# Splitting the last output piece by token stream and starting layer 1 with the latent tokens

## The chip, the cores and the metric

The kernel runs on one core of one Trainium2 chip. The metric is the device time of one execution in microseconds (us). The engines are named as the profile names them: PE (TensorE, matmuls), PEld (its weight loads), DVE (VectorE), ACT (ScalarE), POOL (GpSimd) and SP (SyncE, which issues nearly all the DMAs). Before the change three executions took 1798.65 to 1802.91 us, median 1800.26 us.

## What is computed

Two layers of a hybrid sequence model over 512 tokens of width 2048: 256 context tokens and 256 latent tokens. In each layer the tokens are normalised and modulated by vectors that come from a condition (`adaLN`, a large weight per layer), projected by one wide weight `w_in` into the inputs of four mixers (S5 state space, Hyena long convolution, retention, gated linear attention "GLA"), mixed, gated, projected back by `w_out` and added to the residual:

```python
for i in range(DEPTH):
    ctx_out = i < DEPTH - 1
    mod_l = silu(c) @ ada_w[i] + ada_b[i];  mod_c = silu(c_ctx) @ ada_w[i] + ada_b[i]
    h_l = rmsnorm(x_l, norm_w[i]) * (1 + sc_l) + sh_l      # 256 latent tokens
    h_c = rmsnorm(x_c, norm_w[i]) * (1 + sc_c) + sh_c      # 256 context tokens
    pl = project(h_l, w_in[i], all segments)
    pc = project(h_c, w_in[i], all segments if ctx_out else CTX_STATE_SEGMENTS)
    ... s5, hyena, retention, gla ...
    x_l = x_l + gt_l * (merged branches of the latents @ w_out[i])
    if ctx_out:
        x_c = x_c + gt_c * (merged branches of the context @ w_out[i])
return rmsnorm(x_l, final_norm_w)
```

In the last layer the context is needed only for the states that the latents start from, so its `gla_q` is not computed, while `s5_u` (512 columns) is computed for all 512 tokens and `gla_q` (256 columns) for the latents.

## The kernel before

**Matmuls in three products.** Each fp32 operand is kept as a high and a low part, and each product is hi·hi, hi·lo and lo·hi. The parts of the weights are made as they stream in: `wpart` (L944 on) loads 256 rows by 256 columns (256 KB) into a buffer `raw` (9 of them) by the DMA queue of SP, ACT casts it to `whi` (L935), and DVE subtracts to get `wlo` (L182); there are 6 buffers each of `whi` and `wlo`. The activations of a layer are 16 tiles of 128 features by 512 tokens, each as high and low part (`hs`).

**Buffers.** `tr` is a pool of 4 scratch tiles: modulated activations before they are split, products of the gate and the residual, and projections on the way to DRAM all take their turn in it. PSUM tiles are `pj` (3 buffers), `pA` and `pB` (2 each, asked for as `pm`), and `pa` (1).

**Last output piece.** `w_out` of layer 0 is done in 8 pieces of 256 columns (c = 0 to 7). A piece has 8 weight parts, and each part is used for 4 blocks of 128 tokens (0 and 1 context, 2 and 3 latent) by 6 matmuls of 256 columns, 192 matmuls in all. The four blocks end together at the last part. Each is multiplied by its gate and added to the residual (DVE, L182), its squares are summed (ACT, L1185), and after the last piece the features 14 and 15 are transposed on PE (L201), the four norm factors are spread over all partitions (`rrow`, L1195 on: DVE makes 4 diagonal tiles `junk`, PE multiplies them with ones), and `make_h` (L1211 on) makes the 16 modulated activation tiles of layer 1, all 512 tokens of a tile before the next.

**Start of layer 1.** `proj_wide` (L989 on) projects `s5_u`: 16 weight parts, each 12 matmuls of 512 columns, into two `pj` and two `pB` tiles. Behind each part, `step(2)` advances the background work `ada_gate(1, 't')` by two loads: 32 loads of 256 KB of `ada_w` in all, each with 4 small matmuls into `pa` (L197). Then come the S5 mixer (`s5_mix`), `gla_q` for the latents (`proj(1)`, 8 parts, 96 matmuls of 256 columns) and `gla_k` for all tokens (`proj(2)`, 512 columns a matmul), then the rest of the layer. While these run, a second background load of `ada_w` by DVE (`ada_el`, tile `acc`) goes on.

**Order.** The program text is not the order on the engines: a list scheduler (`schedule_with_timeline_sim=True`, L1610) builds the kernel with a model of its times and lays down one order for each engine, as the pools and the dependences permit. Each engine then runs its own row in order. A buffer of a pool is handed out in the order of the program text, whatever the scheduler does later.

The functions that the change touches are these.

Of the kernel before, what the change touches and what calls it, by code (L numbers as in the profile page):

```python
# [10 lines left out]
F32 = mybir.dt.float32  # L11
# [3 lines left out]
OP = mybir.AluOpType  # L15
# [101 lines left out]
class Net:  # L117
# [826 lines left out]
    def wpart(self, src, r0, c0, w, step=True, keep=False):  # L944

        raw = self.raw()[:, :, :w]
        self.nc.sync.dma_start(raw, src[r0:r0 + 256, c0:c0 + w].rearrange("(k p) c -> p k c", p=128))
        if keep:
            hi, lo = (self.tp.tile([128, 2, 256], F32R, name="m" + t, tag="m" + t, bufs=NM[t])[:, :, :w] for t in 'AB')
        else:  # L950
            hi, lo = self.whl('whi')[:, :, :w], self.whl('wlo')[:, :, :w]
        self.nw += 1
        self.split(hi, lo, raw, 'v')
        if step:
            self.due += self.rate
# [30 lines left out]
            for j in range(2):  # L986
                cb(a // 128 + j, ps[j])

    def proj_wide(self, W, c0, cb, steps):  # L989

        mark(f'pw@{c0}')
        self.cur, cur = 'B', self.cur
        ps = [self.pj(), self.pj(), self.pm(), self.pm()]
# [5 lines left out]
        for j in range(4):  # L999
            cb(j, ps[j])  # L1000

    def proj_n(self, W, c0, w, toks, cb, banks=None, order=range(8), step=True, keep=False):

        mark(f'pn{len(toks)}@{c0}')
        per = 1 if keep else 512 // w
        banks = [b() for b in banks or [self.pj] * (-(-len(toks) // per))]
        parts = {}

        def part(nq):
            if nq not in parts:  # L1010
                parts[nq] = self.wpart(W, order[nq] * 256, c0, w, step, keep)
# [24 lines left out]


    def silu_c(self):
# [157 lines left out]
    def rrow(self, rs):  # L1196
# [49 lines left out]
    def spill(self, dst, t0, scale=None):  # L1246
        def f(j, p):
            x = self.trt()
            if scale:
                self.nc.scalar.mul(x[:, t0:], p[:, t0:], scale)  # L1250
            else:
                self.cp(x[:, t0:], p[:, t0:], EV[j % 2])
            self.nc.sync.dma_start(dst[j * 128:(j + 1) * 128, t0:], x[:, t0:])
        return f

# [159 lines left out]

    WKQ = (0, 1, 6, 7, 4, 5, 2, 3)

    def w_out(self, i, c, toks, t0, x, gt, ss, step=True, done=None):

        cs = slice(c % 2 * 256, (c % 2 + 1) * 256)  # L1420
        mark(f'wout{i}')
# [1 line left out]
        def res(t, p):  # L1423
# [4 lines left out]
            self.sumsq(ss[:, t], c, xx)  # L1428
            if done:
                done(t)  # L1430
        self.proj_n(self.I['w_out'][i], c * 256, 256, toks, res, order=self.WKQ, step=step, keep=bool(done))

    def run(self, out):
        nc, I, tc = self.nc, self.I, self.tc
# [70 lines left out]
        for c in range(8):  # L1505
# [26 lines left out]
        rrow = self.rrow(self.rstd(ss))  # L1532
# [8 lines left out]
        self.layer(1, vec[1], Ps[1], kfd[1], lambda: nxt.update({0: self.gate_row(1, 0, 0)}))  # L1541
        x2 = {}

        def xl(t, c):
# [69 lines left out]
```

## Time and profile before

| | |
|---|---|
| three executions | 1798.65, 1800.26, 1802.91 us |
| the profiled execution | 1800.95 us |
| its span (first to last instruction) | 1799.1 us |
| mean granted clock of PE | 0.984 |
| busy: PE, DVE, ACT, POOL | 1728.2, 1234.9, 739.1, 127.0 us |
| DMA moved | 355.20 MB, mean 197 GB/s |

A row of the page or of an answer about the trace names an operation as line, engine, operation and `out<-in`, with sizes as partitions by elements. PE works for 96% of the span, so a stretch is read by where PE does not work, and by the clock that it is granted: 1.00 stands for 2.4 GHz, 0.50 for 1.2 GHz. Matmuls overlap in their records (a matmul of 256 columns has a duration of 0.28 us, and 252 in a row take 29.91 us), so costs are taken from stretches with a count and not from single durations. The profile is of one execution.

### The profile page before, as it was taken

What the parts mean: (1) busy time and instruction counts of PE and PEld (TensorE: products, weight loads), DVE (VectorE), ACT (ScalarE), POOL (GpSimd) and SP (SyncE); (2) the same over time, 40 slices, a digit from 0 to 9 for tenths busy, and PEclk for the clock granted to TensorE, in tenths of its full rate; (3) what the DMA queues carried; (4) which work ended last, traced back from release to release, by engine and by line L of the source; (5) the groups of instructions that cost most, each with busy time, mean ns of one, the idle gap of its engine ahead of it and who ended that gap; (6) DMA issues with size and microseconds to landing.
All of it is one profiled execution on the core that took longest, in us unless ns stands there. A gap on an engine that the chain in (4) does not pass through costs nothing.

```text
span 1799.1 us, 33742 instructions
## 1 busy us (share of the span) xinstructions
PE 1728.2 (96%) x12560; PEld 1416.5 (79%) x12560; DVE 1234.9 (69%) x2495; ACT 739.1 (41%) x1460; POOL 127.0 (7%) x200
## 2 busy tenths in 40 slices
PE   7997999999999999999899999899999999999997
PEld 4654668888776667876689899777897888999997
DVE  2462876568997784976697564368867688677764
ACT  5331235245336344231242433334355565554554
POOL 4001000000000000000022122000000000000133
PEclk9999999999999999999999999999999999999999
DMA  9766666557556476676885564449654345887963
GB/s 300 247 214 171 204 190 204 162 171 217 166 173 200 144 256 207 208 219 217 300 250 170 145 153 151 141 140 301 211 154 124 106 118 154 268 269 227 317 204 124
DMA packets 308029, 355.20 MB, mean 197 GB/s; under 512 B 42432, under 2 KB 227480, under 8 KB 307864
## 3 DMA queue, kind: packets, MB, share of 16 engines
q1 hardware_dynamic: 299936, 341.81, 62.3%
q10 hardware_dynamic: 5112, 8.79, 1.6%
q0 software_dynamic: 2816, 2.43, 0.7%
q8 instruction: 99, 1.62, 0.4%
q14 instruction: 66, 0.54, 0.1%
HBM read 316.11 MB, written 36.83 MB: 196 GB/s over the span
## 4 chain that ended last, share of the span: by engine, by line
PE 78%; DMA 11%; DVE 5%; ACT 2%; issue 1%; SPq 1%; POOL 0%; DVEq 0%; ACTq 0%; POOLq 0%
PE pj L197 32%; PE pj L1020 21%; PE pB L197 10%; PE pA L197 7%; DMA raw<-in_w_in_dram 4%; PE pa L197 4%; DMA raw<-in_ada_w_dram 2%; PE pB L201 2%; DVE mA L182 1%; PE pA L864 1%; DVE wlo L182 1%; PE pB L1020 1%; DMA kd<-mA 1%; DMA mA<-kd 1%; PE pA L201 1%
## 5 line engine op out<-in xcount | busy, mean ns | idle before, releaser
L197 PE MATMUL pj<-hs,whi 128*128 128x512 f32 (+1 forms) x2496 | 669.9, 355 | 4.4 <-ACT tr L175 3.7
L935 ACT CAST whi<-raw 128x512 fp32r<-128x512 f32 (+1 forms) x536 | 331.5, 621 | 699.2 <-DMA raw<-in_w_in_dram 329.9
L182 DVE TENSOR_TENSOR wlo<-raw,whi 128x512 fp32r<-128x512 f32 (+1 forms) x536 | 373.6, 703 | 302.6 <-ACT whi L935 286.7
L197 PEld LDWEIGHTS pj<-hs,whi 128*128 128x128 f32 x2496 | 432.3, 190 | 86.9 <-issue 21.5
L1020 PE MATMUL pj<-whi,hs 128*128 128x256 f32 (+1 forms) x2368 | 453.7, 289 | 1.2 <-DVE hs L182 1.2
L197 PE MATMUL pj<-hs,wlo 128*128 128x512 f32 (+1 forms) x1248 | 437.0, 353 | 0.2 <-DVE wlo L182 0.2
L1020 PEld LDWEIGHTS pj<-whi,hs 128*128 128x128 f32 x2368 | 372.1, 190 | 17.7 <-issue 15.6
L1020 PE MATMUL pj<-wlo,hs 128*128 128x256 f32 (+1 forms) x1184 | 338.5, 286 | 0.0
L197 PEld LDWEIGHTS pj<-hs,wlo 128*128 128x128 f32 x1248 | 236.4, 190 | 39.3 <-issue 10.0
L1020 PEld LDWEIGHTS pj<-wlo,hs 128*128 128x128 f32 x1184 | 224.5, 190 | 5.7 <-issue 5.2
L182 DVE TENSOR_TENSOR mA<-mA 128x512 f32<-128x512 f32 (+6 forms) x342 | 181.3, 558 | 29.2 <-DMA mA<-rq 12.6
L194 DVE SCALAR_TENSOR_TENSOR acc<-raw,sc,acc 128x512 f32<-128x512 f32 x210 | 153.6, 753 | 10.4 <-DMA raw<-in_ada_w_dram 9.8
L197 PE MATMUL pA<-mA 128*64 128x64 f32 (+4 forms) x892 | 123.2, 302 | 2.9 <-DMA mA<-in_s_glu_w_dram 1.7
L197 PE MATMUL pB<-hs,whi 128*128 128x512 f32 x320 | 104.4, 408 | 9.6 <-ACT whi L935 9.6
L197 PE MATMUL pa<-raw,sc 128*32 128x256 f32 (+1 forms) x1152 | 99.2, 369 | 9.8 <-DMA raw<-in_ada_w_dram 7.8
L197 PE MATMUL pB<-mB 64*64 64x128 f32 (+4 forms) x896 | 95.6, 297 | 10.0 <-DVE mB L182 7.7
L197 PEld LDWEIGHTS pA<-mA 128*64 128x64 f32 (+2 forms) x892 | 75.7, 161 | 26.7 <-issue 13.9
L197 PEld LDWEIGHTS pB<-mB 64*64 64x64 f32 (+2 forms) x896 | 61.5, 154 | 32.1 <-issue 12.3
L175 ACT COPY mA<-pA 128x512 f32<-128x512 f32 (+3 forms) x126 | 50.2, 420 | 88.7 <-PE pA L197 42.2
L197 PEld LDWEIGHTS pa<-raw,sc 128*32 128x32 f32 x1152 | 36.9, 110 | 59.3 <-issue 34.4
L197 PEld LDWEIGHTS pB<-hs,whi 128*128 128x128 f32 x320 | 60.3, 192 | 28.6 <-ACT whi L935 11.0
L182 DVE TENSOR_TENSOR mB<-mB 128x512 f32<-128x512 f32 (+2 forms) x140 | 65.6, 508 | 18.0 <-ACT mB L299 12.2
(230 smaller groups left out, 1587.6 us busy)
## 6 DMA issues: line engine op xcount, KB each, us to landing
raw<-in_ada_w_dram SPq DMA_DIRECT2D x384, 256.0 KB, 3.8
raw<-in_w_in_dram SPq DMA_DIRECT2D x384, 256.0 KB, 3.6
raw<-in_w_out_dram SPq DMA_DIRECT2D x128, 256.0 KB, 3.3
raw<-in_w_in_dram SPq DMA_DIRECT2D x32, 272.0 KB, 3.5
mB<-kfd SPq DMA_DIRECT2D x24, 256.0 KB, 4.8
mB<-in_ctx_dram SPq DMA_DIRECT2D x16, 256.0 KB, 5.5
mB<-in_x_dram SPq DMA_DIRECT2D x16, 256.0 KB, 6.0
kfd<-mA SPq DMA_DIRECT2D x16, 256.0 KB, 2.7
```

Source lines behind the costliest of these rows:

```text
L175: self.nc.scalar.copy(out, in_)
L182: (self.nc.vector if eng == 'v' else self.nc.gpsimd).tensor_tensor(out, a, b, op=op)
L194: self.nc.vector.scalar_tensor_tensor(out, in0, scalar, in1, op0=op0, op1=op1)
L197: self.nc.tensor.matmul(out, lhsT, rhs, start=start, stop=stop)
L201: self.nc.tensor.transpose(out, in_, self.K['ident'][:p, :p])
L864: nc.tensor.matmul(o, a_, b_, start=part == 0 and q < per, stop=part == 2, skip_group_check=True)
L935: self.nc.scalar.copy(hi, x)
L1020: mm = lambda a, b, start, stop: self.nc.tensor.matmul(o, a, b, start=start, stop=stop, skip_group_check=per > 1)
```

## The change

The piece c = 7 of `w_out` of layer 0 is done in two groups of token blocks, first 2 and 3 (latent), then 0 and 1 (context). Its 8 weight parts are kept for the second group: two of them in `mA` tiles of another pool, six in the `whi` and `wlo` buffers. After each group `half` does the transposes, the norm factors and `rrow` for these 256 tokens. The scale vectors of all 16 features are made in one instruction (`acols`), ahead of the piece.

Layer 1 begins with `proj_lat` on the latents: in each of 8 rounds two parts of `s5_u` and one of `gla_q`, 12 matmuls of 256 columns each (288 in all), with no background loads, and with the modulation of two features for the latents (`make_h_part`) at the round's start. Then `proj_lat` does `s5_u` for the context: 8 rounds of two parts (192 matmuls of 256 columns), the modulation for the context, and two background loads behind each part. So the 16 weight parts of `s5_u` are loaded and split twice. The results go to four tiles `ux` by ACT copies, and from there to DRAM; `proj(1)` is gone, its result is spilled at the end of the latent phase.

```diff
-    def proj_wide(self, W, c0, cb, steps):
...
+    def proj_lat(self, W, units, steps, before, ts):
...
+        ps = [self.pj() if ts.start else self.pm() for _ in units]
...
         for kq in range(8):
-            for a in range(2):
-                self.proj_part(W, kq, c0 + a * 256, ps[2 * a:2 * a + 2], 0, kq == 0, kq == 7, False)
+            before(kq)
+            for (c0, j0, cb), p in zip(units, ps):
+                hi, lo = self.wpart(W, kq * 256, c0, 256, False)
+                for j in range(2):
+                    cs = slice(j * 128, (j + 1) * 128)
+                    o = p[:, j * 256:(j + 1) * 256]
...
+                    for k in range(2):
+                        xh, xl = self.hh[kq * 2 + k][:, ts], self.hl[kq * 2 + k][:, ts]
+                        mm(hi[:, k, cs], xh, kq == 0 and k == 0 and j == 0, False)
+                        mm(hi[:, k, cs], xl, False, False)
+                        mm(lo[:, k, cs], xh, False, kq == 7 and k == 1)
                 self.step(steps)
...
-        for nq in range(8):
-            for n in range(len(toks)):
-                block(nq, n)
-        for n in range(len(toks)):
-            out(n)
+        groups = [range(len(toks))] if half is None else [range(0, 2), range(2, 4)]
+        for ns in groups:
+            for nq in range(8):
+                for n in ns:
+                    block(nq, n)
+            for n in ns:
+                out(n)
+            if half:
+                half(ns[0] // 2)
...
+    def make_h_part(self, k, x, m, acols, rrow, v, ts):
...
+        f = self.trt()
+        f = f[:, ts]
+        self.stt(f, x[:, ts], acols[:, k, v:v + 1], rrow[:, ts], op0=OP.mult, op1=OP.mult)
...
+        self.nc.scalar.activation(hi, f, AF.Identity, bias=b)
+        self.stt(lo, f, b, hi.bitcast(F32), op0=OP.add, op1=OP.subtract)
...
-            self.proj_wide(W, OFF[units[0][0]], units[0][3], 2)
+            ux = [self.t2() for _ in range(4)]
+            part = lambda ts: lambda j, p: self.cp(ux[j][:, ts], p)
+            two = lambda cb: [(OFF['s5_u'] + a, a // 128, cb) for a in (0, 256)]
+            self.proj_lat(W, two(part(slice(256, 512))) + [(OFF['gla_q'], 0, units[1][3])], 0, before_lat, slice(256, 512))
+            self.proj_lat(W, two(part(slice(0, 256))), 2, before_ctx, slice(0, 256))
+            for j in range(4):
+                units[0][3](j, ux[j])
         self.cur = 'A'
         self.s5_mix(i, P, vec, self.ud, lat, put)
         if lat:
-            proj(1)
             proj(2)
...
+        def half(h):
+            toks = (2, 3) if h == 0 else (0, 1)
...
+            for k in (14, 15):
+                p = self.pm()
+                for n, t in enumerate(toks):
+                    self.tr(p[:, n * 128:(n + 1) * 128], x1[t, 3][:, (k % 4) * 128:(k % 4 + 1) * 128])
...
+            self.rrow_part(rrow, sl[h], self.rstd(ss[:, toks[0]:toks[1] + 1]))
...
+        self.w_out(0, 7, (2, 3, 0, 1), 0, x0, gt, ss, False, half=half)
         self.hh, self.hl = [], []
-        for k in range(KT):
-            self.make_h(k, xT[k], m[1], vec[1], rrow)
+
+        def before(h):
+            def f(kq):
+                for k in (2 * kq, 2 * kq + 1):
+                    self.make_h_part(k, xT[k], m[1], ac, rrow, h, sl[h])
+            return f
```

Up to the piece c = 7 the two kernels lay the same instructions in the same order, but for the scale vectors. Behind it, all of layer 1 is scheduled anew. Three places follow, before first and then after; line numbers of the changed kernel are its own.

PE at the end of the piece, before: the last `w_out` matmuls, then background matmuls (`pa`), the transposes (L201), the norm factors (`junk`), and the first matmuls of `s5_u` on 512 tokens.

```order
L1020 MATMUL pj<-wlo,hs 128x256
L1020 MATMUL pj<-whi,hs 128x256
L197 MATMUL pa<-raw,sc 32x256 x16
L201 MATMUL pB<-c_kc,mB 128x128 x4
L197 MATMUL pa<-raw,sc 32x256 x2
L201 MATMUL pB<-c_kc,mB 128x128 x2
L197 MATMUL pa<-raw,sc 32x256 x2
L201 MATMUL pB<-c_kc,mB 128x128 x2
L197 MATMUL pa<-raw,sc 32x256 x4
L197 MATMUL pA<-junk,c_kc 128x128 x4
L197 MATMUL pa<-raw,sc 32x256 x6
L197 MATMUL pj<-hs,whi 128x512 x2
```

PE at the same place now: the last context matmuls of the piece, the context's transposes, and the first matmuls of `s5_u` on 256 latents; L1031 is in `w_out`, L1002 in `proj_lat`.

```order
L1031 MATMUL pj<-whi,hs 128x256 x2
L1031 MATMUL pj<-wlo,hs 128x256
L1031 MATMUL pj<-whi,hs 128x256
L201 MATMUL pB<-c_kc,mB 128x128 x4
L1002 MATMUL pj<-hs,whi 128x256 x4
L1002 MATMUL pj<-hs,wlo 128x256
L1002 MATMUL pj<-hs,whi 128x256 x2
L1002 MATMUL pj<-hs,wlo 128x256
```

The background matmuls and the latents' transposes and factors stand no longer between the piece and layer 1; the latter lie inside the context group of the piece.

DVE at the end of the piece, before: the products of gate and residual (`tr<-pj,mA`), the sums (`mB<-mB,tr`), the norm factors and the modulation (`tr<-mB,acol,mA`).

```order
L182 TENSOR_TENSOR mB<-mB,tr 128x256
L182 TENSOR_TENSOR tr<-pj,mA 128x256
L182 TENSOR_TENSOR mB<-mB,tr 128x256
L177 COPY mB<-pB 128x512
L182 TENSOR_TENSOR wlo<-raw,whi 128x2x256
L1191 TENSOR_REDUCE xs_12040<-xss 128x4
L239 RECIPROCAL xrs<-xrs 128x4
L1201 TENSOR_SCALAR junk<-c_kc,xrs 128x128 x4
L194 SCALAR_TENSOR_TENSOR tr<-mB,acol,mA 128x256 x8
L194 SCALAR_TENSOR_TENSOR acol<-mod_147,vec 128x2
L194 SCALAR_TENSOR_TENSOR hs<-tr,mod_147,hs 128x256 x2
```

DVE at the same place now.

```order
L177 COPY mA<-pB 128x256
L182 TENSOR_TENSOR wlo<-raw,whi 128x2x256 x5
L182 TENSOR_TENSOR tr<-pj,mA 128x256
L182 TENSOR_TENSOR mB<-mB,tr 128x256
L182 TENSOR_TENSOR wlo<-raw,whi 128x2x256
L182 TENSOR_TENSOR tr<-pj,mA 128x256
L182 TENSOR_TENSOR mB<-mB,tr 128x256
L194 SCALAR_TENSOR_TENSOR tr<-mB,acols,mA 128x256 x3
L177 COPY mA<-pB 128x256
L1206 TENSOR_REDUCE xs_12060<-xss 128x2
L194 SCALAR_TENSOR_TENSOR tr<-mB,acols,mA 128x256
L194 SCALAR_TENSOR_TENSOR hs<-tr,mod_147,hs 128x256 x2
```

The modulation of the latents still begins behind the products and sums of the last token block; it is no longer behind the context's norm factors.

SP's DMA queue around the boundary, before: residual loads, then two loads of `ada_w` (L1063) for each weight part (L947).

```order
L1502 DMA mB<-in_ctx_dram 128x512 x2
L1502 DMA mB<-in_x_dram 128x512 x2
L1063 DMA raw<-in_ada_w_dram 128x512 x2
L947 DMA raw<-in_w_in_dram 128x2x256
L1063 DMA raw<-in_ada_w_dram 128x512 x2
```

SP at the same place now (L1078 loads `ada_w`).

```order
L1553 DMA mB<-in_x_dram 128x512 x2
L947 DMA raw<-in_w_in_dram 128x2x256 x6
L1593 DMA x1d<-mB 128x512 x2
L947 DMA raw<-in_w_in_dram 128x2x256 x16
L1078 DMA raw<-in_ada_w_dram 128x512 x2
L947 DMA raw<-in_w_in_dram 128x2x256
L1078 DMA raw<-in_ada_w_dram 128x512 x2
```

The 24 parts of the latent phase and one of the context phase are asked for first (some of the 16 and 6 rows), and the 32 background loads all stand among the 16 parts of the context phase, two by two.

ACT near the end of the projection `ret_v` of layer 1, before: activations of S5 and GLA with their table loads, a weight cast (L935), then the copies of `ret_v` out of PSUM (`tr<-pj`).

```order
L810 ACT_TABLE_LOAD
L810 ACTIVATE mA<-mA,hpi 128x256
L316 ACT_TABLE_LOAD
L316 ACTIVATE mB<-mB 128x256
L317 ACTIVATE mB<-mB 128x256
L935 CAST whi<-raw 128x2x256
L312 ACTIVATE mB<-mB 128x512
L175 COPY tr<-pj 128x256 x4
```

ACT at the same place now.

```order
L316 ACT_TABLE_LOAD
L316 ACTIVATE mB<-mB 128x256
L317 ACTIVATE mB<-mB 128x256
L312 ACTIVATE mB<-mB 128x512
L935 CAST whi<-raw 128x2x256 x2
L175 COPY mB<-pB 128x512
L935 CAST whi<-raw 128x2x256
L175 COPY mA<-pA 128x128
L935 CAST whi<-raw 128x2x256
L175 COPY mA<-pA 128x128
L175 COPY tr<-pj 128x256 x4
```

Four weight casts and three copies now stand between the activations and the copies of `ret_v`.

## Rows read from the trace of the kernel before

**Rows 1.** Windows at the boundary; columns: busy us per engine, PEclk, DMA share, GB/s.

```profile
1132.30:1155.97 23.67, 23.67 (x204) 23.54 (x207) 6.56 (x11) 8.09 (x19) 2.07 (x3) 1.00 0.30 87
1155.97:1174.11 18.14, 12.54 (x93) 5.36 (x93) 12.80 (x37) 7.72 (x21) 0.00 (x0) 0.91 0.85 274
1174.11:1222.12 48.01, 48.01 (x247) 36.42 (x245) 27.72 (x70) 18.32 (x39) 0.00 (x0) 1.00 0.45 135
1222.12:1240.52 18.40, 15.63 (x141) 14.34 (x138) 17.22 (x30) 6.29 (x13) 0.00 (x0) 0.91 0.99 321
```

**Rows 2.** Timeline of PE there: start, us, work, [idle before it and what ended it].

```profile
1163.64 0.63 PE L197 MATMUL pa<-raw,sc 128*32 128x256 f32 x4 [1.72 <-DMA raw<-in_ada_w_dram]
...
1167.98 1.21 PE L197 MATMUL pa<-raw,sc 128*32 128x256 f32 x8 [1.37 <-DMA raw<-in_ada_w_dram]
...
1170.96 1.22 PE L197 MATMUL pj<-hs,whi 128*128 128x512 f32 x2
```

**Rows 3.** Windows of 2 us there, columns as before.

```profile
1170.00:1172.00 2.00, 2.00 (x7) 1.00 (x8) 2.00 (x8) 1.08 (x3) 0.00 (x0) 0.50 1.06 369
1172.00:1174.00 2.00, 2.00 (x15) 0.75 (x13) 2.00 (x8) 0.00 (x0) 0.00 (x0) 0.67 0.78 270
```

**Rows 4.** Timeline of PE in the attention q stretch.

```profile
1230.77 0.41 PE L197 MATMUL pA<-mA,cbr 64*32 64x128 f32 x4 [1.77 <-DVE mA L182]
...
1240.52 0.63 PE L197 MATMUL pj<-hs,whi 128*128 128x512 f32 x2
```

**Rows 5.** Windows of 2 us in that stretch.

```profile
1230.00:1232.00 2.00, 1.03 (x7) 0.76 (x8) 2.00 (x5) 0.00 (x0) 0.00 (x0) 0.84 0.97 311
1232.00:1234.00 2.00, 2.00 (x10) 1.87 (x10) 2.00 (x4) 0.62 (x1) 0.00 (x0) 0.50 1.05 343
```

**Rows 6.** Chain of waits, two stretches: start, us, work and count.

```profile
1184.58 2.79 PE pj L197 x12
...
1207.65 1.00 PE pa L197 x16
...
1667.95 29.91 PE pj L197 x252
```

**Rows 7.** Window of the 252 matmuls of the last row above.

```profile
1667.95:1697.86 29.91, 29.91 (x255) 29.91 (x254) 21.69 (x46) 15.90 (x32) 0.43 (x1) 1.00 1.00 320
```

**Rows 8.** Timeline of DVE after the last output matmuls.

```profile
1157.14 0.42 DVE L182 TENSOR_TENSOR mB<-mB,tr 128x256 f32<-128x256 f32 x1
1157.48 0.42 DVE L182 TENSOR_TENSOR tr<-pj,mA 128x256 f32<-128x256 f32 x1
```

**Rows 9.** Groups by line from 1155.97 to 1240.52: busy us, mean ns | idle before, releasers.

```profile
L182 DVE TENSOR_TENSOR wlo<-raw,whi 128x512 fp32r<-128x512 f32 x22 | 15.0, 686 | 23.1 <-ACT whi L935 15.9 <-PE pB L197 7.3
...
L194 DVE SCALAR_TENSOR_TENSOR hs<-tr,mod,hs 128x256 fp32r<-128x256 f32 x32 | 14.0, 476 | 0.0
L1225 ACT ACTIVATE hs<-tr,mod 128x256 fp32r<-128x256 f32 x32 | 13.6, 497 | 3.9 <-DVE tr L194 3.9
L935 ACT CAST whi<-raw 128x512 fp32r<-128x512 f32 x22 | 13.6, 620 | 47.7 <-DMA raw<-in_w_in_dram 32.8 <-PE pj L197 6.1 <-DVE acc L194 5.9
...
L197 PE MATMUL pa<-raw,sc 128*32 128x256 f32 x128 | 11.8, 398 | 5.2 <-DMA raw<-in_ada_w_dram 5.2
```

**Rows 10.** Timeline of PE at the end of retention v.

```profile
1481.61 0.80 PE L197 MATMUL pj<-hs,whi 128*128 128x256 f32 x2 [3.67 <-ACT tr L175]
```

**Rows 11.** Timeline of ACT there.

```profile
1466.46 0.69 ACT L296 ACTIVATE mB<-pB,vec 128x512 f32<-128x512 f32 x1 [2.30 <-PE pB L197]
...
1468.66 1.28 ACT L299 ACT_TABLE_LOAD   x1
1469.95 0.63 ACT L299 ACTIVATE mB<-mB 128x512 f32<-128x512 f32 x1
...
1480.93 1.17 ACT L175 COPY tr<-pj 128x256 f32<-128x256 f32 x4
```

**Rows 12.** Window behind that wait.

```profile
1480.00:1490.00 10.00, 8.39 (x49) 8.39 (x49) 8.70 (x15) 5.59 (x12) 0.00 (x0) 0.66 0.56 159
```

More of the change, by code (lines that the diff above doesn't have):

```diff
@@ L948, in wpart @@
         if keep:
-            hi, lo = (self.tp.tile([128, 2, 256], F32R, name="m" + t, tag="m" + t, bufs=NM[t])[:, :, :w] for t in 'AB')
+            hi, lo = (self.tp.tile([128, 2, 256], F32R, name="m" + t, tag="m" + t, bufs=NM[t])[:, :, :w] for t in keep)
         else:
@@ L987, in proj_t, with proj_n @@
                 cb(a // 128 + j, ps[j])
-    def proj_wide(self, W, c0, cb, steps):
-        mark(f'pw@{c0}')
+    def proj_lat(self, W, units, steps, before, ts):
+        mark('plat')
         self.cur, cur = 'B', self.cur
-        ps = [self.pj(), self.pj(), self.pm(), self.pm()]
+        ps = [self.pj() if ts.start else self.pm() for _ in units]
         self.cur = cur
         for kq in range(8):
-            for a in range(2):
-                self.proj_part(W, kq, c0 + a * 256, ps[2 * a:2 * a + 2], 0, kq == 0, kq == 7, False)
+            before(kq)
[4 more added lines that the diff above has]
+                    o = p[:, j * 256:(j + 1) * 256]
+                    mm = lambda a, b, start, stop: self.nc.tensor.matmul(o, a, b, start=start, stop=stop, skip_group_check=True)
+                    for k in range(2):
[3 more added lines that the diff above has]
+                        mm(lo[:, k, cs], xh, False, kq == 7 and k == 1)
                 self.step(steps)
-        for j in range(4):
-            cb(j, ps[j])
-    def proj_n(self, W, c0, w, toks, cb, banks=None, order=range(8), step=True, keep=False):
+        for (c0, j0, cb), p in zip(units, ps):
+            for j in range(2):
+                cb(j0 + j, p[:, j * 256:(j + 1) * 256])
+    def proj_n(self, W, c0, w, toks, cb, banks=None, order=range(8), step=True, keep=False, half=None):
         mark(f'pn{len(toks)}@{c0}')
@@ L1010, in part @@
             if nq not in parts:
-                parts[nq] = self.wpart(W, order[nq] * 256, c0, w, step, keep)
+                parts[nq] = self.wpart(W, order[nq] * 256, c0, w, step, 'AB' if keep else 'AA' if half and nq < 2 else '')
             return parts[nq]
@@ L1205, in rrow, with rrow_part, acols @@
         return x
+    def rrow_part(self, x, ts, rs):
+        n = ts.stop - ts.start
+        p = self.pm()
+        for t in range(n // 128):
+            d = self.sm.tile([128, 128], F32, name="junk")
+            self.nc.vector.tensor_scalar(d, self.K['ident'], rs[:, t:t + 1], None, op0=OP.mult)
+            self.mm(p[:, t * 128:(t + 1) * 128], self.K['ones'], d)
+        self.cp(x[:, ts], p[:, :n])
+    def acols(self, m, vec):
+        a = self.sm.tile([128, 16, 2], F32, name="acols", bufs=1)
+        self.stt(a, m[:, 1], 1.0, vec[:, 0:16, None].to_broadcast([128, 16, 2]), op0=OP.add, op1=OP.mult)
+        return a
+    def make_h_part(self, k, x, m, acols, rrow, v, ts):
+        mark('makeh')
+        f = self.trt()
+        f = f[:, ts]
+        self.stt(f, x[:, ts], acols[:, k, v:v + 1], rrow[:, ts], op0=OP.mult, op1=OP.mult)
+        if len(self.hh) <= k:
+            self.hh.append(self.hs())
+            self.hl.append(self.hs())
+        hi, lo = self.hh[k][:, ts], self.hl[k][:, ts]
+        b = m[:, 0, k, v:v + 1]
+        self.nc.scalar.activation(hi, f, AF.Identity, bias=b)
+        self.stt(lo, f, b, hi.bitcast(F32), op0=OP.add, op1=OP.subtract)
     def warm_sqrt(self, ss):
@@ L1416, with w_out @@
     WKQ = (0, 1, 6, 7, 4, 5, 2, 3)
-    def w_out(self, i, c, toks, t0, x, gt, ss, step=True, done=None):
+    def w_out(self, i, c, toks, t0, x, gt, ss, step=True, done=None, half=None):
         cs = slice(c % 2 * 256, (c % 2 + 1) * 256)
@@ L1430, in res @@
                 done(t)
-        self.proj_n(self.I['w_out'][i], c * 256, 256, toks, res, order=self.WKQ, step=step, keep=bool(done))
+        self.proj_n(self.I['w_out'][i], c * 256, 256, toks, res, order=self.WKQ, step=step, keep=bool(done), half=half)
     def run(self, out):
@@ L1510, in run @@
                 self.warm_sqrt(ss)
+                break
             self.w_out(0, c, range(4), 0, x0, gt, ss, c < CS)
@@ L1540, in run @@
         self.bg = self.ada_gate(1, HOW[6:8])
-        self.layer(1, vec[1], Ps[1], kfd[1], lambda: nxt.update({0: self.gate_row(1, 0, 0)}))
+        self.layer(1, vec[1], Ps[1], kfd[1], lambda: nxt.update({0: self.gate_row(1, 0, 0)}),
+                   before(0), before(1))
         x2 = {}
```

23 lines of the change are left out of this document (19 added, 4 removed).

## The prediction

> **What bounds the kernel now.** I read first the share of PE (96% of the span), then windows around the place that the change touches, then PE's timeline there, then the chain of waits. The windows [rows 1] show four stretches. Up to 1155.97 us, the end of the last `w_out` matmuls, PE is full. In the next 18.14 us, from the residual to the first matmuls of `s5_u`, PE has 12.54 us of busy records at a mean clock of 0.91. Then come 48.01 us full at clock 1.00, and 18.40 us with `gla_q` in which PE has 15.63 us, DVE 17.22 us and the DMAs a share of 0.99. Everything else of layer 1 keeps its amount of work.
>
> How much of these 84.55 us is lost? Matmuls are priced by counted rows [rows 6]: 252 of 256 columns in 29.91 us are 0.1187 us each, 12 of 512 columns in 2.79 us are 0.2325, 16 background ones in 1.00 us are about 0.065. The work is 192 × 0.2325 = 44.6 for `s5_u`, 96 × 0.1187 = 11.4 for `gla_q`, 128 × 0.065 = 8.3 for the background [rows 9], and my estimate of 3.1 for transposes, factors and pieces of S5: 67.4 us. So about 17 us are lost: some 11 in the first stretch, where PE waits for loads of `ada_w` (1.72 and 1.37 us [rows 2]) that stand ahead of weights in SP's queue and then runs two windows at 0.50 and 0.67 [rows 3]; some 5 in the `gla_q` stretch, where a wait of 1.77 us on DVE's S5 work [rows 4] is followed by windows at 0.84 and 0.50 [rows 5]; 1 elsewhere.
>
> **The change, part by part.** I count from the same point, the last `w_out` matmul, to the first matmul of `gla_k`, which was at 1240.52 [rows 4].
>
> *The piece by halves.* It has the same 192 matmuls, and the latents' transposes and factors go into the context half, where PE is full (0.7 us of PE). But the modulation of the latents does not start there: its scratch tile comes from the pool of 4 that the residual products also use, so in DVE's order the first one stands behind the last context sum. What the change seems made to hide stays open. From the last matmul: products and sums of two blocks at 0.79 a block (0.34 + 0.45, from one add to the next [rows 8]) and a weight split at about 0.6 make 2.2; one modulation on DVE 0.48 and the high part on ACT 0.50 [rows 9] make 3.2; the low part, behind two more DVE instructions, adds 0.8. That is a gap of 4.0 us. Bounds: 2.8 if the first block's residual is done while the second still multiplies, 6 if the low parts come one by one behind all scratch copies.
>
> *Clock behind the gap.* After the wait of 1.77 us the clock cost about 1.3 us (0.32 + 1.0 in two windows [rows 5]), after a wait of 3.67 us 3.4 us (10 us at 0.66 [rows 10, 12]). The gap is nearest to the second: 3.4.
>
> *Latent phase.* 288 × 0.1187 = 34.2 us. Beside it, per round of 36 matmuls (4.3 us): DVE three splits at 0.69 and four modulation steps at 0.48, 4.0 us; ACT three casts at 0.62 and two high parts at 0.50, 2.9 us [rows 9]. DVE is close, but the records overlap by about a tenth, and the first parts are prepared during the piece, so I cost the cover as holding. If it doesn't, the phase is 2 us longer. 24 loads of 262 kB in 34 us are 185 GB/s, and no load of `ada_w` stands among them.
>
> *Context phase.* PE has 192 × 0.1187 = 22.8 and 128 × 0.065 = 8.3, 31 us. But all 32 background loads now stand here, two behind each of 16 weight parts; before, they had the 64 us from 1157 to 1222. The 9 `raw` buffers bound what can be fetched ahead: by the order, some 13 of the 48 loads (eight of `ada_w`, and weights that were already cast) when the latent phase ends, since `pa` matmuls stand behind it on PE. The other 35 come at the rate of a saturated stretch, 320 GB/s [rows 7], 0.82 us each: 28.7 us. PE's own start costs about 2.8 us more, since ACT has four copies and the spill of `gla_q` ahead of the next cast and a scratch tile waits for the store; and the last load needs its landing, cast and split. I take 37 us. Bounds: 31 (PE alone decides) and 42 (the 274 GB/s of the second stretch [rows 1]: 35 × 0.96 = 33.5, and the same ends).
> The Trainium skill ("DMA: Bandwidth & Descriptors", Specifications) gives about 358 GB/s as a core's limit to its memory. By that the 35 loads would take an estimated 25.6 us and the phase end 3 us earlier. The saturated stretch shows 320 [rows 7], with 256 KB loads like these, and I keep to that.
>
> *Behind it.* The S5 input is complete some 12 us later than before. Its mixer is spread over the layer beside PE, and the long run of 252 matmuls at 1667.95 [rows 6] shows work that fills PE late, so I cost it at nothing; if that cover fails, it is part of the slower case. The S5 pieces that stood in the `gla_q` stretch (1.7 us) now come after `gla_k` begins and count in both. The doubled splits (16 casts, 16 subtractions) lie beside matmuls.
>
> The sum: 4.0 + 3.4 + 34.2 + 37 = 78.6, and 1.7 for the S5 pieces and 1.2 for transposes and factors that are done in both make 81.5, against 84.55: 3.1 us gained. In this the smaller matmuls cost 480 × 0.1187 − 44.6 − 11.4 = 1.0 us.
>
> *A stall far behind.* At the end of `ret_v` PE waits 3.67 us [rows 10] for copies by ACT that stand behind a block of S5 and GLA activations with five table loads, from 1466.46 to 1480.93 [rows 11], and the clock then costs 3.4 us [rows 12]. Now the copies stand farther behind that block, and PE has about 135 matmuls between the one that starts the block and the one that needs the copies, against 9.7 us before the wait: some 16 to 20 us, longer than the 14.5 us of the block. Then 7.1 us go. But all of the layer is laid anew, and another block may meet another wait: 0 to 7.1, and I take half, 3.5.
>
> Together 3.1 + 3.5 = 6.6 us. The profiled execution is 1800.95 us (span 1799.1), 0.7 above the median of 1800.26. 1800.95 − 6.6 = 1794.3 us.
>
> **Rivals.**
> *Faster than that* (1789 us): the context phase is bounded by PE alone (31 us, 6 less). For it: the DMAs idle at a share of 0.45 in the stretch of 48 us [rows 1] and may run further ahead. Against: nine buffers. Chance 0.13.
> *No change* (1800 us): the context phase takes 42 us and the stall of ACT only moves: 3.1 − 5 + 3.5 = 1.6 with half of it, −1.9 with none, about 0 between. For it: every stretch here that mixes `ada_w` with weights has PE waiting [rows 2, 5]. Against: the long stretch does not. Chance 0.26.
> *Slower* (1806 us): PE stops for loads of `ada_w` once in each round of the context phase, and the clock falls again and again. Rows 3 and 5 show 0.50 behind waits of 1.4 to 1.8 us. With half of the phase's 31 us of work at 1.2 GHz, that half takes 15 us more; about 3.5 of it covers waits that were there anyway, so 12 us are added. It decides as soon as most rounds have a wait of over 1.4 us, which 37 us against 31 does not yet give (6 us over 16 parts are 0.4 each). The Trainium skill ("TensorE: Matmul & The Clock Gate", HAM oscillation) tells of a loop in which short bursts of matmuls between waits for loads slow the clock in every turn; the windows here agree that the clock falls behind such waits, and no row shows it in turn after turn. Chance 0.17, with a new ACT collision or a late S5 counted in it.
> *Not what it says*: the overlap of modulation and context half does not happen, which is already in the sum.
>
> **How the numbers follow.** Forecast 0.44, faster rival 0.13, no change 0.26, slower 0.17. A measurement tells changes from about 0.2% (3.6 us). Faster by more: the faster rival, nearly all of the forecast (0.41 of 0.44) and a little of no change (0.02), 0.56. Within: 0.26 with 0.03 from the forecast, less 0.04 to the sides, 0.25. Slower: 0.19. The forecast's own range is 1790 to 1798 (terms 28.7 to 33.5, 0 to 7.1); reaching to the middle of the faster and the slower case it becomes 1787 to 1805.
>
> **What would show it.** Right: one gap of PE of about 4 us between the last `w_out` and the first latent matmul, then windows at 0.50; a full latent phase of 34 us; a context phase of about 37 us with the DMA share near 1.00, about 320 GB/s and PE's waits on loads of `ada_w` under 1 us; `gla_k` some 3 us earlier; no wait of 3 us on an ACT copy of `ret_v`. Wrong: a gap under 2 us (the overlap works after all) or a second wait between the phases; windows at 0.50 inside the context phase; PE full there; or a difference that grows behind `gla_k`, which would put the cause into the new order of the layer.

## The result and the profile after

The changed kernel is slower: 1813.2 us median of nine executions (1809.74 to 1819.31) against 1800.26 (nine, 1795.26 to 1810.3), ratio 1.0074 (95% interval 1.0055 to 1.0092), some 13 us. The forecast was 1794.3 us with a range of 1787 to 1805. The profiled execution has a span of 1807.9 us against 1799.1.

The last `w_out` matmul of layer 0 ends at a different point in each profile (here 1152.02, before 1155.97), so I count from its start, 1151.74 and 1155.69 us, and cut there and at the first matmul of `gla_k` (1234.04 and 1240.52): 82.3 us now against 84.8 before in the front, 573.9 against 558.6 behind it. The front gained 2.5 us, and 15.3 us were lost behind it, 12.8 us together. (The two spans differ by 8.8 us only, because up to that matmul the changed kernel's profile was already 4.0 us ahead.)

Windows of the changed kernel: the gap, the latent phase, the context phase, and the clock behind the gap (columns as in [rows 1]).

```profile
1152.02:1155.70 3.68, 0.85 (x4) 0.40 (x4) 3.57 (x9) 2.40 (x8) 0.00 (x0) 1.00 0.71 194
1155.70:1192.75 37.05, 36.59 (x292) 36.25 (x292) 27.39 (x58) 21.52 (x43) 0.00 (x0) 0.95 0.55 151
1192.75:1234.04 41.29, 40.16 (x322) 28.17 (x321) 21.54 (x45) 18.26 (x36) 0.00 (x0) 1.00 0.88 282
...
1156.00:1158.00 2.00, 1.54 (x11) 1.34 (x10) 2.00 (x7) 1.07 (x4) 0.00 (x0) 0.86 0.01 3
1158.00:1160.00 2.00, 2.00 (x11) 2.00 (x11) 2.00 (x7) 1.32 (x3) 0.00 (x0) 0.50 0.00 0
1160.00:1162.00 2.00, 2.00 (x16) 2.00 (x15) 2.00 (x6) 1.63 (x4) 0.00 (x0) 0.79 0.01 4
```

Behind the last output piece some 7 us were lost before: of 18.14 us PE was not busy for 5.6 [rows 1], and the clock cost 1.7 [rows 3]. Now there are a gap of 3.7 us and a slow clock that costs 1.7 us (0.28 + 1.00 + 0.42 over three windows). The latent phase is full. So is the context phase, nearly, at clock 1.00: not the DMAs bound it, but PE, which is busy for 40.2 of its 41.3 us. The background matmuls are the reason. Less 192 × 0.1187 = 22.8 us for `s5_u`, 17.4 us are left for 128 of them. Their own records (`pa` alone in that window) cover 14.63 us:

```profile
1192.75:1234.04 41.29, 14.63 (x128) 4.17 (x128) 0.00 (x0) 0.00 (x0) 1.00 0.88 282
```

The loss behind `gla_k` is one of waiting. Windows from `gla_k` to the first `w_out` of layer 1, before and after:

```profile
1240.52:1697.70 457.18, 449.71 (x3862) 404.88 (x3861) 346.82 (x670) 239.91 (x463) 4.17 (x20) 0.99 0.66 196
```

```profile
1234.04:1707.54 473.50, 452.76 (x3902) 407.21 (x3901) 361.89 (x696) 245.73 (x475) 5.26 (x20) 0.99 0.67 198
```

PE is not busy for 7.5 us of it before, of which 3.67 are the wait of [rows 10], and for 20.7 us in the changed kernel. Its waits there (us in total, times, longest):

```profile
PE pj L197 <- ACT tr L1454: 10.2, 1, 10.2
PE pA L864 <- DMA mA<-kd: 3.7, 3, 2.5
PE pB L201 <- DVE mB L182: 2.3, 1, 2.3
PE pA L201 <- DVE mA L182: 1.3, 1, 1.3
...
PE pj L197 <- ACT tr L175: 0.3, 1, 0.3
```

The stall at `ret_v` is gone, as forecast (0.3 us at most is left of the 3.67). But one wait of 10.2 us stands at the last gates (L1454). Its links, from the timelines of ACT, DVE, SP and PE of the changed kernel:

```profile
1666.10 0.32 SPq L1281 DMA_DIRECT2D ys<-mA  x1
...
1667.55 8.77 SPq L1433 DMA_DIRECT2D mA<-ys  x16
...
1672.59 2.37 DVE L182 TENSOR_TENSOR mA<-mA,mB 128x256 f32<-128x256 f32 x4 [7.48 <-DMA mA<-ys]
...
1675.39 0.78 ACT L1454 ACTIVATE tr<-pj 128x256 f32<-128x256 f32 x2 [8.01 <-DVE mA L194]
...
1675.83 0.79 PE L197 MATMUL pj<-hs,whi 128*128 128x256 f32 x2 [10.16 <-ACT tr L1454]
```

Read upwards: PE waits for a PSUM tile that ACT has to empty; ACT waits for one of the four `tr` tiles; DVE, which uses them up, waits for mixer outputs (`ys`) to come back from DRAM; and all 16 reloads stand in SP's queue behind the last store of retention, at 1666.10. Hyena's last store was already issued by then (`ys<-mB`):

```profile
1664.22 0.79 SPq L1281 DMA_DIRECT2D ys<-mB  x2
```

In the kernel before, on SP:

```profile
1653.46 0.41 SPq L1236 DMA_DIRECT2D ys<-mA  x1
...
1655.91 0.43 SPq L1382 DMA_DIRECT2D mA<-ys  x1
...
1660.38 4.59 SPq L1382 DMA_DIRECT2D mA<-ys  x9
...
1667.44 0.34 SPq L1236 DMA_DIRECT2D ys<-mB  x1
...
1676.03 0.42 SPq L1236 DMA_DIRECT2D ys<-mB  x1
```

There, too, all 16 reloads stand behind retention's last store. But that store, at 1653.46, comes 16.6 us earlier, counted from the last `w_out` matmul (497.8 against 514.4 us), and Hyena was not done: 12 reloads went out ahead of its last four stores (1667.44 to 1676.03), while it still gave PE work. Back along the chain, the first DRAM store of the S5 mixer (`kd<-mA`, L788), before and after:

```profile
1239.92 0.38 SPq L788 DMA_DIRECT2D kd<-mA  x1
```

```profile
1259.54 0.47 SPq L788 DMA_DIRECT2D kd<-mA  x1
```

From the last `w_out` matmul that is 84.2 us before and 107.8 us after. Before, S5 began while `gla_q` still ran, so that `gla_q` covered its first steps; now `gla_q` is done and S5's input is complete only with the context phase. On PE that input is complete 15.9 us later than before (82.3 against 66.4 us), and the first store comes 23.6 us later.

### The profile page after: what moved, and what is told of

Read it like the earlier page. It is cut to its first block, busy times and chain, and to the rows that moved or that the text cites. A ratio compares the mean times of both kernels' runs of the same rounds, so it can differ in the third digit from the quotient of the medians.

```text
span 1807.9 us, 34226 instructions
## 1 busy us (share of the span) xinstructions
PE 1730.2 (96%) x12752; PEld 1425.0 (79%) x12752; DVE 1247.0 (69%) x2499; ACT 754.3 (42%) x1488; POOL 126.7 (7%) x200
## 4 chain that ended last, share of the span: by engine, by line
PE 77%; DMA 10%; DVE 6%; ACT 3%; issue 2%; SPq 1%; POOL 0%; DVEq 0%; ACTq 0%; POOLq 0%
PE pj L197 30%; PE pj L1031 20%; PE pB L197 9%; PE pA L197 7%; PE pa L197 5%; DMA raw<-in_w_in_dram 4%; DVE mA L182 2%; PE pj L1002 2%; PE pB L1002 1%; DVE wlo L182 1%; DMA raw<-in_ada_w_dram 1%; PE pB L1031 1%; PE pA L864 1%; PE pB L201 1%; PE pA L201 1%
## 5 line engine op out<-in xcount | busy, mean ns | idle before, releaser
L197 PE MATMUL pj<-hs,whi 128*128 128x512 f32 (+1 forms) x2368 | 634.1, 355 | 12.0 <-ACT tr L1454 10.2
L935 ACT CAST whi<-raw 128x512 fp32r<-128x512 f32 (+1 forms) x550 | 339.8, 621 | 663.7 <-DMA raw<-in_w_in_dram 299.1
L182 DVE TENSOR_TENSOR wlo<-raw,whi 128x512 fp32r<-128x512 f32 (+1 forms) x550 | 385.8, 707 | 293.0 <-ACT whi L935 279.0
L197 PEld LDWEIGHTS pj<-hs,whi 128*128 128x128 f32 x2368 | 411.1, 191 | 91.0 <-issue 19.4
L1031 PE MATMUL pj<-whi,hs 128*128 128x256 f32 (+1 forms) x2336 | 445.4, 287 | 0.0
L197 PE MATMUL pj<-hs,wlo 128*128 128x512 f32 (+1 forms) x1184 | 416.0, 355 | 0.0
L1031 PEld LDWEIGHTS pj<-whi,hs 128*128 128x128 f32 x2336 | 365.2, 189 | 14.3 <-issue 13.1
L1031 PE MATMUL pj<-wlo,hs 128*128 128x256 f32 (+1 forms) x1168 | 332.2, 285 | 0.0
L197 PEld LDWEIGHTS pj<-hs,wlo 128*128 128x128 f32 x1184 | 224.7, 190 | 37.0 <-issue 9.0
L1031 PEld LDWEIGHTS pj<-wlo,hs 128*128 128x128 f32 x1168 | 219.9, 188 | 4.9 <-issue 4.7
L182 DVE TENSOR_TENSOR mA<-mA 128x512 f32<-128x512 f32 (+6 forms) x342 | 181.1, 559 | 27.9 <-DMA mA<-rq 10.2
L194 DVE SCALAR_TENSOR_TENSOR acc<-raw,sc,acc 128x512 f32<-128x512 f32 x210 | 154.2, 756 | 11.0 <-DMA raw<-in_ada_w_dram 10.3
L175 ACT COPY mA<-pA 128x512 f32<-128x512 f32 (+2 forms) x125 | 49.6, 420 | 101.7 <-PE pA L197 56.1
L197 PE MATMUL pB<-hs,whi 128*128 128x512 f32 x256 | 83.9, 412 | 6.8 <-ACT whi L935 6.8
L197 PEld LDWEIGHTS pB<-hs,whi 128*128 128x128 f32 x256 | 48.4, 194 | 23.3 <-ACT whi L935 8.2
```

What stands on the lines that cost most here:

```text
L175: self.nc.scalar.copy(out, in_)
L182: (self.nc.vector if eng == 'v' else self.nc.gpsimd).tensor_tensor(out, a, b, op=op)
L194: self.nc.vector.scalar_tensor_tensor(out, in0, scalar, in1, op0=op0, op1=op1)
L197: self.nc.tensor.matmul(out, lhsT, rhs, start=start, stop=stop)
L935: self.nc.scalar.copy(hi, x)
```

## The experiments

Theory A: S5 and retention follow one another (both take their scratch from `mA`, in program order), this chain is nearly critical in the kernel before, and the change starts it late. Theory B: only the new order of the reloads on SP is at fault. Theory C: the front itself costs the time. Theories D (a late S5 costs the same whatever the delay) and E (the background loads bind the context phase) came up on the way. For each kernel the time from the last `w_out` matmul (its start) to the end is split at S5's first store and at retention's last store, each from its own profile:

| kernel | to S5's first store | S5 and retention | from there to the end | sum | ratio to before (interval) |
|---|---|---|---|---|---|
| before | 84.2 | 413.5 | 145.6 | 643.4 | 1 |
| after | 107.8 | 406.6 | 141.8 | 656.2 | 1.0074 (1.0055 to 1.0092) |
| b_qfirst | 116.5 | 404.7 | 143.8 | 665.0 | 1.0112 (1.0083 to 1.0140) |
| b_qkfirst | 134.9 | 424.4 | 140.9 | 700.2 | 1.0328 (1.0292 to 1.0365) |
| a_qlast | 93.8 | 415.3 | 143.2 | 652.4 | 1.0050 (1.0029 to 1.0070) |
| a_ysq | 108.3 | 408.1 | 132.0 | 648.4 | 1.0020 (1.0001 to 1.0039) |
| a_steps | 107.9 | 416.7 | 140.3 | 664.9 | 1.0174 (1.0145 to 1.0204) |
| a_cut | 108.7 | 327.2 | 191.2 | 627.1 | 0.9922 (0.9895 to 0.9950) |
| b_cut | 83.6 | 342.0 | 206.8 | 632.4 | 0.9944 (0.9925 to 0.9964) |
| b_half | 78.8 | 414.4 | 147.7 | 640.9 | 0.9979 (0.9957 to 1.0000) |
| b_half_again | 80.2 | 415.6 | 147.0 | 642.8 | 0.9976 (0.9960 to 0.9993) |
| bh_ysq | 78.7 | 416.6 | 146.6 | 641.9 | 0.9977 (0.9959 to 0.9995) |
| bh_s1 | 69.8 | 425.7 | 148.8 | 644.3 | 1.0004 (0.9982 to 1.0025) |

b_half and b_half_again are one kernel, so a sum is good to some 2 us. What lies ahead of the last `w_out` matmul is in the ratios but not in the sums; it took 1149 to 1169 us in these profiles.

**b_qfirst**: S5 late without the split.

```diff
+            proj(1)
             self.proj_wide(W, OFF[units[0][0]], units[0][3], 2)
...
-            proj(1)
             proj(2)
```

> The kernel before, with gla_q projected ahead of s5_u instead of behind it: the same work, no split by streams, but the S5 mixer's input is complete some 18 us later against the start of gla_k. Theory A (the changed kernel lost its time because S5 starts late, the chain S5 then retention ends late, and PE runs out of other work before the last gates): S5's first store comes 15 to 20 us after the start of gla_k instead of at it, PE waits 5 to 12 us near the end of layer 1, and the time is 1805 to 1813 us, ratio 1.003 to 1.007. Theory B (only the order of the SP queue at the end is at fault, all 16 reloads of mixer outputs standing behind retention's last store; S5's lateness is innocent): in this kernel 12 of the reloads stand ahead of Hyena's last stores as before, so no long wait and 1797 to 1803 us, ratio 0.998 to 1.002.

Ratio 1.0112, more than A said. S5's first store comes 26 us behind the start of `gla_k`, and the part behind that start takes 574.7 us, as in the changed kernel (573.9). PE waits at the last gates though the reloads stand in nearly the old order (12 of them ahead of Hyena's last two stores):

```profile
1682.05 0.79 PE L197 MATMUL pj<-hs,whi 128*128 128x256 f32 x2 [6.67 <-ACT tr L1403]
```

B alone falls. The front costs 5.4 us besides (90.2 us), which I had not expected.

**a_qlast**: the split stays, `gla_q` back behind S5.

```diff
-            self.proj_lat(W, two(part(slice(256, 512))) + [(OFF['gla_q'], 0, units[1][3])], 0, before_lat, ...
+            self.proj_lat(W, two(part(slice(256, 512))), 0, before_lat, ...
...
+            proj(1)
             proj(2)
```

> The changed kernel, with gla_q taken out of the latent phase and projected behind the S5 mixer as before; the split by streams and the halved output piece stay. Theory A: S5's first store comes about at the start of gla_q, some 10 us earlier against the rest than in the changed kernel, retention's last store comes early enough, the wait of 10.2 us near the end shrinks to under 3 us, and the time is 1796 to 1803 us, ratio 0.998 to 1.002. Theory C (the front itself costs the time, by doubled splits and shorter matmuls): it stays at 1809 to 1814 us, ratio 1.005 to 1.008.

The time missed A's range, 1.0050. The part behind `gla_k`'s start (counted from where `gla_q` is done; two matmuls of `gla_k` stand ahead of that) is as A said, 557.3 us (558.6 before), and the wait at the gates is gone (4.1 us stand elsewhere). But the front takes 95.1 us, 10.3 more than before: a context phase of 42.2 us and a `gla_q` stretch of 22.6 us, of which PE is not busy for 4.8. So C holds for this kernel: without `gla_q` in the latent phase the split pays nothing and costs 10 us. In the table this loss, too, goes with S5's start: it is 9.6 us later than before, and the sum is 9.0 us larger.

Four kernels now differ only in whether they have the change's front and in where `gla_q` stands. With `gla_q` ahead of S5 the part behind `gla_k`'s start takes 574.7 us (old front) and 573.9 (new); with `gla_q` behind S5's input it takes 558.6 (old) and 557.3 (new). In the first two S5's first store comes some 26 us behind the start of `gla_k`, in the other two about 1 us ahead of it. So what is lost behind `gla_k` goes with S5's lateness and not with the split.

**a_ysq**: reloads off SP.

```diff
-            nc.sync.dma_start(o, self.ys[k, :, :n])
+            (nc.gpsimd if lat else nc.sync).dma_start(o, self.ys[k, :, :n])
```

> The changed kernel, with the reloads of the mixer outputs of layer 1 issued on GpSimd's DMA queue instead of SP's, so that they stand behind no weights and behind no store of another queue. Theory B: the reloads of S5 and GLA outputs land long before they are needed, the wait of 10.2 us falls under 1 us, and the time is 1798 to 1802 us, ratio 0.999 to 1.001. Theory A: the gates of S5 and GLA can go on, but retention still ends some 12 us later than before, so a wait of 3 to 8 us comes at retention's gates, and the time is 1803 to 1809 us, ratio 1.002 to 1.005. Theory C: 1809 to 1814 us.

Ratio 1.0020: the wait at the gates falls to 2.2 us, and retention's last store is followed by 132.0 us instead of 141.8.

```profile
PE pj L197 <- ACT tr L1454: 2.2, 1, 2.2
```

S5 and retention are as late as in the changed kernel. So the order of the queue turned lateness into about 8 us of the loss by the sums (10 by the ratios), and the late chain keeps the rest. The ratio lies at the lower end of A's range, and the interval reaches down into B's; the wait is between what the two said.

**b_half**, and once more **b_half_again**: only the output piece in halves (`w_out(0, 7, ..., half=half)`), then `make_h` and `proj_wide` as before.

> The kernel before, with only the last output piece done in two halves (latents first, norm factors by halves); layer 1 begins as before with the projection of s5_u for all 512 tokens. It tells what the halves do alone. Theories A and B: the modulation still waits for all tokens, S5 starts where it did, so the front gains 0 to 3 us and the tail stays: 1796 to 1801 us, ratio 0.998 to 1.000. Theory C: doubled splits are not in it, so 1797 to 1801 us as well; above 1805 us the halves themselves would be at fault.

> The kernel before with only the last output piece in halves, once more, because its interval reached 1.000. Theory A and B: ratio 0.996 to 1.000, front 81 to 83 us, S5's first store 78 to 80 us behind the last output matmul. Noise alone: ratio 0.999 to 1.002.

Ratios 0.9979 and 0.9976, the second with an interval below 1: about 4 us faster than the kernel before, and by the two intervals 0 to 8 (the sums show 0.6 to 2.5); with bh_ysq it is the fastest version here that leaves nothing out. The front takes 81.6 and 81.2 us (to where `gla_q` is done), less than in the changed kernel (82.3), and S5 starts at 79 to 80 us. What the front gained, the halves had gained alone.

**b_qkfirst**: `gla_k` as well ahead of `s5_u` (`proj(1)`, `proj(2)`, then `proj_wide`).

> The kernel before, with both gla_q and gla_k projected ahead of s5_u: the same work, S5's input complete another 22 us later than with gla_q alone ahead (96 matmuls of 512 columns at 0.2325 us). Theory A as a sum (the time from the last output matmul of layer 0 to the end is: to S5's first store, plus 405 to 415 us of S5 and retention one behind the other, plus 143 us from retention's last store to the end; this held within 3 us for five of the kernels so far): 139 + 405 + 143 = 687 us against 643 before, so 1840 to 1848 us, ratio 1.020 to 1.026. Rival D (a late S5 costs once, by the order that the scheduler then lays, about 15 us whatever the delay): as with gla_q alone ahead, 1815 to 1826 us, ratio 1.009 to 1.014.

D falls: 1.0328. The loss grows with the delay, and by more than A's sum and range, 700.2 us instead of 687: the chain itself took 424 us, outside the 405 to 415 of the others. Hyena's last store is at 1655.60 here and retention's at 1717.38, so retention runs alone at the end, with waits of PE on its DVE steps and at the gates (from 1660 us on):

```profile
PE pA L197 <- DVE mA L182: 20.3, 4, 9.8
PE pj L197 <- ACT tr L1402: 9.1, 1, 9.1
PE pA L201 <- DVE mA L182: 4.6, 2, 2.3
```

**a_cut** and **b_cut**: the fourth S5 block of layer 1 left out, a shorter chain.

```diff
-            U = self.t2()
+            if not lat_only or b < 3:
+                U = self.t2()
...
```

> The changed kernel, with the fourth of the four S5 blocks of layer 1 left out (its result is a copy of the third's), so that the chain S5 then retention is some 70 to 80 us shorter. To be read against the kernel before with the same left out, beside it. Theory A: the chain no longer ends last, the wait of 10.2 us at the last gates is gone, and this kernel takes 0 to 4 us less than the other cut one (the front's gain of 2.5 us remains). Rivals C and D: it takes 9 to 15 us more than the other cut one, as without the cut.

> The kernel before, with the fourth S5 block of layer 1 left out in the same way. The matmuls and waits of that block go, 3 to 12 us by all theories: 1788 to 1797 us, ratio 0.993 to 0.998. It is the reference for the changed kernel with the same cut.

With 79 and 72 us less of chain, 191 and 207 us are left behind it: it no longer ends last. The changed kernel then is not slower than the other: 0.9922 against 0.9944, with overlapping intervals; by their ends it loses at most 4.5 us, where it lost 13 uncut. In neither does the profile show a wait of PE between 1500 and 1700 us. With the four kernels above this is the strongest evidence for A: the same front, the same doubled splits, and no loss.

**a_steps**: one background load behind each part of both phases.

```diff
-            self.proj_lat(W, ... + [(OFF['gla_q'], 0, units[1][3])], 0, before_lat, slice(256, 512))
-            self.proj_lat(W, two(part(slice(0, 256))), 2, before_ctx, slice(0, 256))
+            self.proj_lat(W, ... + [(OFF['gla_q'], 0, units[1][3])], 1, before_lat, slice(256, 512))
+            self.proj_lat(W, two(part(slice(0, 256))), 1, before_ctx, slice(0, 256))
```

> The changed kernel, with one background load behind each weight part in the latent and the context phase (24 and the rest) instead of two in the context phase alone. Theory A: S5 starts at most 2 us earlier, the front takes 80 to 84 us, and the late chain still costs 13 to 17 us behind it: 1809 to 1817 us, ratio 1.005 to 1.009. The prediction's view, that the context phase is bound by 32 background loads (rival E): the context phase falls from 41 us to 33 to 36 us, the latent phase grows by 2 us, S5 starts 4 to 6 us earlier: 1804 to 1809 us, ratio 1.002 to 1.005.

Neither: 1.0174. The front is 81.2 us, 1.1 less, and S5 starts no earlier, so E falls. The context phase did shrink, from 41.3 to 28.7 us, by more than E said, but the latent phase grew from 37.1 to 46.5 and the gap ahead of it from 4.0 to 6.0: the background matmuls cost PE time wherever they stand (7.5 of the 9.4 us more in the latent phase are busy time, 1.9 waiting). Latent and context phase of a_steps:

```profile
1174.63:1221.12 46.49, 44.10 (x371) 38.45 (x369) 26.01 (x54) 20.94 (x43) 0.00 (x0) 0.95 0.69 211
1221.12:1249.83 28.71, 28.55 (x219) 25.58 (x217) 25.74 (x52) 16.23 (x33) 0.00 (x0) 0.96 0.94 301
```

The chain took 10 us longer than in the changed kernel, and PE waits three times on retention near the end:

```profile
PE pj L197 <- ACT tr L1454: 9.0, 1, 9.0
PE pA L197 <- DVE mA L182: 8.0, 2, 7.6
PE pA L201 <- DVE mA L182: 2.3, 1, 2.3
```

The sum is 21.5 us above that before, while the measured ratio means 31; some 10 us lie ahead of layer 1. Up to the last `w_out` matmul, a_steps and then the changed kernel:

```profile
0.00:1168.60 1168.60, 1118.92 (x7468) 870.29 (x7468) 771.36 (x1599) 418.17 (x823) 94.92 (x146) 0.98 0.65 197
```

```profile
0.00:1151.74 1151.74, 1108.20 (x7467) 861.81 (x7468) 772.08 (x1599) 418.03 (x823) 91.00 (x146) 0.99 0.66 200
```

The same instructions in the same order on PE, DVE and ACT took 16.9 us longer: PE was busy for 10.7 us more, at a clock of 0.98 instead of 0.99, and not busy for 6.1 us more. The experiment changes nothing there but loads that SP issues near its end (from 1112 us on). So some 10 us of the ratio are probably not its doing; where they come from is open.

**bh_ysq** and **bh_s1**: the halves with the reloads on GpSimd's queue, and with one background load a part.

> The kernel before with the last output piece in halves, and the reloads of the mixer outputs of layer 1 on GpSimd's DMA queue: a candidate that should beat both kernels. Theory A: the chain S5 then retention starts 79 us behind the last output matmul and is not last by much, the separate queue takes a few us off what follows retention's last store (it took 10 us off in the changed kernel, 141.8 to 132.0), but PE is nearly full there, so 0 to 4 us are left to gain over the halves alone: 1792 to 1799 us, ratio 0.994 to 0.998. Theory B (the queue's order is worth about 8 us in any kernel): 1788 to 1792 us, ratio 0.991 to 0.993.

> The kernel before with the last output piece in halves, and one background load of the gate weights behind each part of s5_u instead of two; the other 16 come later, beside gla_q, gla_k and the S5 mixer. Theory A: S5's input is complete 1 to 4 us earlier, since 64 background matmuls and their waits leave the front, and the end follows only as far as PE has work: ratio 0.995 to 1.000. Rival: as with the background loads moved in the changed kernel (ratio 1.017 there), moving them lengthens S5's chain by about 10 us: ratio 1.003 to 1.010.

The separate queue gives nothing beyond the halves (0.9977): where the chain isn't late, the order of the reloads costs nothing that can be measured here. That falls in A's range, and B's is missed. With one load a part S5 starts 9 us earlier, but the chain takes 426 us and nothing is gained: 1.0004, just above A's range. I read it so that from that side the chain stretches beside PE's work, which then is the bound; no run tests that.

## Why the prediction was wrong

- *What was lost before.* I had 17 us of the 84.55. PE was not busy for 5.6 and 2.8 us of the two broken stretches [rows 1], and the clock, at 0.91 in both, cost 3.3: some 12 us. The rest was work that I had priced too low, the background matmuls above all (below).
- *The gap.* Forecast 4.0 us, measured 3.7 from the end of the last matmul and 4.0 from its start (1151.74 to 1155.70). As read from the order, the modulation came behind the last context sum.
- *The clock behind it.* Forecast 3.4, measured 1.7: it was nearer that of the 1.77 us wait [rows 4, 5] than of the 3.67 us one. PE's transposes stood in the gap, which was three waits of 1.07, 0.90 and 0.87 us.
- *The latent phase.* 34.2 and the clock's 1.7 are 35.9; measured 37.1, with a wait of 0.46 and the context's factors in it.
- *The context phase.* Forecast 37 us, bound by loads; measured 41.3, bound by PE. The term that was mis-sized is the background: 128 matmuls cost 17.4 us (0.136 each) and not 8.3 (0.065), so PE alone has 40.2 us and not 31. My price came from 16 in a row [rows 6]; here most come in fours between others. The landing rate of 282 GB/s at a share of 0.88 stayed below that of [rows 7], so the case does not say whether the limit of the Trainium skill ("DMA: Bandwidth & Descriptors", Specifications) or that row is nearer.
- *The sum of the front.* Forecast 3.1 us of gain, measured 2.5. That is luck: 4.3 us too little for the context phase stand against 1.7 and 1.2 that I had added for S5 pieces and transposes and that do not come on top in this stretch, and 0.9 too much for the gap and the latent phase.
- *The stall at `ret_v`.* Counted at half of 7.1; it went whole.
- *Behind it: the step that failed.* The S5 input comes later; "Its mixer is spread over the layer beside PE, and the long run of 252 matmuls at 1667.95 [rows 6] shows work that fills PE late, so I cost it at nothing". The run of 252 matmuls is work, but it is that of the gates themselves: their results leave PSUM through the `tr` tiles, and those come free only when a reload has come. It can't cover a wait for the reloads. What covers a late chain is work that PE may do before retention ends, and that ran out. From `gla_k` to the first `w_out` of layer 1 PE took 16.3 us more (473.5 against 457.2): 13.3 in which PE is not busy, net of the stall that went, and 3.0 of work, mostly 40 matmuls of S5 that stood ahead of `gla_k` before. b_qfirst and b_qkfirst show that a late S5 alone does this, a_cut that nothing does it once the chain is short, and a_ysq that about 8 us of it came by way of SP's order. The delay was mis-sized as well: "some 12 us later" was 15.9 us on PE and 23.6 at S5's first store. Two of my signs of being wrong came true, PE full in the context phase and "a difference that grows behind `gla_k`", which did point to the cause.
- *The rivals.* My slower case gave the right side by the wrong way: the clock did not fall in the context phase (1.00), where PE waited for 1.1 us in all. No round-by-round slowing as in the Trainium skill ("TensorE: Matmul & The Clock Gate", HAM oscillation) was seen there. "A late S5" stood in it as an aside without a price. It has one: the delay is 24 us, the chain of S5 and retention ended 146 us before the end of the kernel before, and the least that is left behind it in any kernel here without the separate queue is 140 us. That leaves an estimated 5 us of slack, which I could have looked for by following the chain back from the last reloads.

What stays open: why the chain takes 405 to 425 us and stretches in a_steps, how much of that is its own latency and how much the scheduler's order, and why nearly the same work ahead of layer 1 differs by up to 19 us between profiles.

## What to carry to other kernels

Where work is reordered at the front of a stage, find the longest chain that its results feed, and ask how long before the end it ends; busy shares say nothing about that. A move that fills PE now, with work that used to cover the start of a serial chain, is paid for when the chain ends. Do the parts of a change one at a time: here the halves alone gave some 4 us, and the rest of the change cost some 17.

## What the runs showed of the hardware

Small matmuls between others cost more than twice what they cost in a row. The context phase of the changed kernel begins with 32 background matmuls in a row:

```profile
1192.75 1.93 PE L197 MATMUL pa<-raw,sc 128*32 128x256 f32 x32
```

That is 0.06 us each, as in [rows 6]. For the other 96, most of them in fours, 15.5 of the phase's 40.16 busy us are left (less 22.8 and 1.93), 0.16 each. One such four in the chain of waits, 0.14 each:

```profile
1224.80 0.56 PE pa L197 x4
```

And the same reordering copy of 512 columns by ACT takes twice as long from an SBUF tile as from PSUM. Groups by line, first the changed kernel, then the kernel before:

```profile
L175 ACT COPY tr<-mA 128x512 f32<-128x512 f32 x4 | 4.8, 1206 | 0.0
```

```profile
L175 ACT COPY tr<-pj 128x512 f32<-128x512 f32 x2 | 1.2, 580 | 0.0
```
